# Attention on one core: score blocks in one stream of groups of three, on two PSUM buffers, with the rest of TensorE's work taken from a list

## The chip, the cores and the metric

One core of a Trainium2 chip. The metric is the device time of one execution in microseconds (us), the median over several executions. Before: 136.06 us (135.83 to 136.16). One profiled execution of each kernel gives the trace; its span is about 1.8 us shorter than the time.

## The reference

```python
batch, heads, seq, dim = 8, 8, 512, 64          # float32 q, k, v
scores = np.einsum('bhqd,bhkd->bhqk', q, k) / np.sqrt(dim)
attn = np.exp(scores - scores.max(-1, keepdims=True))
attn = attn / attn.sum(-1, keepdims=True)
return np.einsum('bhqk,bhkd->bhqd', attn, v)
```

There are 64 heads, handled as 32 pairs. Each pair has 8 score blocks of 128 keys x 512 queries (4 chunks of keys, 2 heads). The kernels leave the maximum out and get the sum from a column of ones beside v.

## The kernel before

In the trace TensorE's work stands in the order in which the program is written: four scores from 92.49 us on, 16 value matmuls from 93.48, four transposes from 94.00, and the next scores from 94.32. Per pair, GpSimd casts q, k, v to fp16, TensorE transposes q and k (into tp), and VectorE copies the result to tqk. Then TensorE makes scores (st), ScalarE takes the exponential (pt; one such instruction is called an activation), TensorE multiplies with v (into the accumulator o), and VectorE normalises (rc, ob). The program puts all that TensorE writes into PSUM memory: three buffers for st, one for tp, one for o.

```python
    ps_st = ... tile_pool(name="ps_st", bufs=3, space=PSUM)   # 3 buffers of 1024 columns
    ps_o  = ... tile_pool(name="ps_o",  bufs=1, space=PSUM)   # 1 buffer
    ps_t  = ... tile_pool(name="ps_t",  bufs=1, space=PSUM)   # 1 buffer
    ...
    def scores(g, half):              # 2 blocks of each head of the pair
        ss = [ps_st.tile([P, 2, S], FP32, tag="st", ...) for h in range(2)]
        # ... four matmuls, each on the 64 rows of its head
        for h in range(2):
            nc.scalar.activation(out=pts[g][h][:, 2*half : 2*half+2, :],
                                 in_=ss[h][:, :, :], func=EXP, scale=scale)
    def values(g, h):                 # 16 matmuls into o, then the normalisation
        o = ps_o.tile([P, NI, D + 1], FP32, tag="o", ...)
        # ... matmuls
        nc.vector.reciprocal(out=rc[:, :, :], in_=o[:, :, D : D + 1])
        nc.vector.tensor_tensor(out=ob[:, h], in0=o[:, :, 0:D],
                                in1=rc[:, :, :].broadcast_to([P, NI, D]), op=AluOp.mult)
    ...
        for g in range(NP):
            load(g + AHEAD); cast(g + 3)
            scores(g + 1, 0)
            values(g, 0)
            transpose(g + 3, 1)
            scores(g + 1, 1)
            values(g, 1)
            transpose(g + 3, 0)
```

The scores of the two heads start almost together: in the trace two at 21.459 and 21.465 us, the next at 21.674.

The softmax here doesn't subtract the row's maximum and nothing guards it: scores larger than these inputs give would overflow.

## Time and profile before

| | before |
|---|---|
| time | 136.06 us |
| span of the profiled run | 134.3 us |
| ScalarE busy | 118.9 us (89%) |
| activations | 128 of 1024 columns |
| activation 4, after eight blocks | starts at 14.43 us |
| last activation | starts at 127.34 us |

To the lines that the prediction shows I add ScalarE's group and all that it waited for. The columns of the first are busy time, mean duration of one in ns, and the idle time in front; those of the second are total wait, number, longest.

```profile
L115 ACT ACTIVATE pt<-st 128x1024 f16<-128x1024 f32 x128 | 117.6, 1261 | 9.0 <-PE st L107 9.0
...
ACT pt L115 <- PE st L107: 9.0, 3, 5.5
```

ScalarE waits three times in the whole run, all before 17 us. After that it is the bound, and only two things can help: fewer microseconds per column on ScalarE, or a shorter head and tail.

### The profile page before, as it was taken

Reading aid. Unit: us, or ns where it says so; the run is one execution under the profiler, and the core shown is the slowest. Engines: PE = TensorE matmul, PEld = TensorE weight load, DVE = VectorE, ACT = ScalarE, POOL = GpSimd, SP = SyncE. Lnnn points to the kernel's source line nnn. Section 1 sums busy time; section 2 is a strip of 40 time slices with the busy share of each in tenths; the row PEclk is TensorE's granted clock in tenths of the full one; section 3 lists DMA queues with packets and bytes.
Section 4 is the critical chain, followed back from the end, with each engine's and each line's share of the span. In section 5 each row is a group of like instructions: output and inputs, shape, how many; then the busy total and the mean of one; then the engine's idle time right before and its main releaser. Section 6 shows DMA issues by size and latency. Waiting matters only on the chain.

```text
span 134.3 us, 3901 instructions
## 1 busy us (share of the span) xinstructions
PE 115.7 (86%) x1536; PEld 61.6 (46%) x1536; DVE 60.4 (45%) x192; ACT 118.9 (89%) x129; POOL 59.9 (45%) x108
## 2 busy tenths in 40 slices
PE   0475999999999999999999999999999999998750
PEld 0223455554445554445554445554445554444340
DVE  0203455445555445554445554445554445553230
ACT  3073599999999999999999999999999999999930
POOL 2578831555355554545516545535537624500000
PEclk9999999999999999999999999999999999999975
DMA  4999937999998999988999969979998879422222
GB/s 127 292 326 358 301 100 230 324 318 267 285 306 293 290 263 295 307 266 302 315 277 284 300 192 307 320 248 314 314 296 305 290 224 289 151 78 78 83 78 78
DMA packets 34835, 33.81 MB, mean 252 GB/s; under 512 B 2049, under 2 KB 34817, under 8 KB 34817
## 3 DMA queue, kind: packets, MB, share of 16 engines
q1 hardware_dynamic: 34816, 33.56, 78.7%
q8 instruction: 12, 0.20, 0.6%
q14 instruction: 7, 0.05, 0.1%
HBM read 25.17 MB, written 8.39 MB: 250 GB/s over the span
## 4 chain that ended last, share of the span: by engine, by line
ACT 64%; issue 15%; PE 12%; DVE 3%; DMA 2%; POOL 0%; ACTq 0%
ACT pt L115 64%; PE st L107 5%; PE o L131 3%; PE tp L92 3%; DMA k<-in_k_dram 2%; DVE tqk L93 2%; DVE ob L140 1%; POOL qkp L78 0%; DVE rc L139 0%; ACTq L115 0%
## 5 line engine op out<-in xcount | busy, mean ns | idle before, releaser
L115 ACT ACTIVATE pt<-st 128x1024 f16<-128x1024 f32 x128 | 117.6, 1261 | 9.0 <-PE st L107 9.0
L107 PE MATMUL st<-tqk 64*128 64x512 f16 x256 | 62.8, 394 | 7.0 <-ACT pt L115 1.6
L131 PEld LDWEIGHTS <-pt 128*128 128x128 f16 x1024 | 36.6, 99 | 28.5 <-DVE tqk L93 24.6
L131 PE MATMUL o<-vp,pt 128*128 128x65 f16 x1024 | 44.5, 196 | 1.6 <-DVE ob L140 1.6
L78 POOL CAST qkp<-k 128x512 f16<-128x512 f32 x32 | 19.6, 613 | 48.8 <-DMA k<-in_k_dram 33.5
L139 DVE RECIPROCAL rc<-o 128x4 f32<-128x4 f32 x64 | 11.6, 182 | 57.1 <-PE o L131 57.1
L93 DVE COPY tqk<-tp 128x512 f16<-128x512 f16 x64 | 26.4, 413 | 11.3 <-PE tp L92 11.3
L92 PE MATMUL tp<-ident,qkp 128*128 128x128 f16 x256 | 26.1, 228 | 6.3 <-POOL qkp L78 4.2
L140 DVE TENSOR_TENSOR ob<-o,rc 128x256 f32<-128x256 f32 x64 | 27.1, 424 | 2.2
L107 PEld LDWEIGHTS <-tqk 64*128 64x128 f16 x256 | 12.3, 94 | 32.5 <-issue 26.4
L83 POOL CAST vp<-v 128x512 f16<-128x512 f32 x32 | 19.7, 616 | 5.8 <-DMA v<-in_v_dram 3.9
L78 POOL CAST qkp<-q 128x512 f16<-128x512 f32 x32 | 19.6, 613 | 2.5 <-DMA q<-in_q_dram 1.9
L92 PEld LDWEIGHTS <-qkp 128*128 128x128 f16 x256 | 16.5, 101 | 7.8 <-POOL qkp L78 4.7
L115 ACT ACT_TABLE_LOAD x1 | 1.3, 1283 | 0.7 <-PEq L194 0.7
masks.py:197 POOL MEMSET ident<- 128x128 f16 x1 | 0.2, 204 | 0.3 <-POOLq L194 0.3
masks.py:199 POOL TENSOR_SCALAR_AFFINE_SELECT ident<-ident 128x128 f16<-128x128 f16 x1 | 0.3, 292 | 0.1
L160 POOL MEMSET vp<- 128x8 f16 x6 | 0.3, 135 | 0.0
L194 POOL MEMSET const-float32-0.0<- 128x1 f32 x1 | 0.1, 98 | 0.2 <-issue 0.2
L194 POOL MEMSET const-bfloat16-1.0<- 128x1 bf16 x1 | 0.1, 101 | 0.0
L194 POOL MEMSET const-uint8-127<- 128x1 uint8 x1 | 0.1, 101 | 0.0
L194 POOL MEMSET const-float32-1.0<- 128x1 f32 x1 | 0.1, 98 | 0.0
## 6 DMA issues: line engine op xcount, KB each, us to landing
k<-in_k_dram SPq DMA_DIRECT2D x32, 256.0 KB, 4.1
q<-in_q_dram SPq DMA_DIRECT2D x32, 256.0 KB, 4.3
v<-in_v_dram SPq DMA_DIRECT2D x32, 256.0 KB, 4.4
out_dram<-ob SPq DMA_DIRECT2D x32, 256.0 KB, 3.2
```

The source lines that it names most:

```text
L78: nc.gpsimd.tensor_copy(out=t[:, n].rearrange("p i (h d) -> p h i d", h=2), in_=tiles[name][:, :, :, :],)
L83: nc.gpsimd.tensor_copy(out=vps[g % NV][:, :, :, 0:D], in_=tiles["v"][:, :, :, :])
L92: nc.tensor.transpose(tp[:, i, :], qkp[g][:, n, i, :], ident)
L93: nc.vector.tensor_copy(out=tqk[g][:, n, :], in_=tp.rearrange("p i c -> p (i c)"))
L107: nc.tensor.matmul(ss[h][:, cc, :], tqk[g][po : po + 64, 1, c * P : (c + 1) * P], tqk[g][po : po + 64, 0, :], start=True, stop=True,)
L115: nc.scalar.activation(out=pts[g][h][:, 2 * half : 2 * half + 2, :], in_=ss[h][:, :, :], func=EXP, scale=scale,)
L131: nc.tensor.matmul(o[:, qc, :], pts[g][h][:, c, qc * P : (qc + 1) * P], vps[g % NV][:, h, c, :], start=(c == 0), stop=(c == NI - 1),)
L139: nc.vector.reciprocal(out=rc[:, :, :], in_=o[:, :, D : D + 1])
L140: nc.vector.tensor_tensor(out=ob[:, h], in0=o[:, :, 0:D], in1=rc[:, :, :].broadcast_to([P, NI, D]), op=AluOp.mult,)
L160: nc.gpsimd.memset(vps[n][:, :, :, D : D + 1], 1.0)
L194: nc = _bacc.Bacc("TRN2", target_bir_lowering=False, num_devices=1)
```

## The change

The intent is to spare ScalarE's fixed cost per instruction: undisturbed activations start 0.903 us apart with 1024 columns (before) and 1.331 us with 1536 (the changed kernel), which can be put as 0.836 ns a column and 47 ns an instruction. The 256 score blocks of all pairs form one stream, cut into groups of three: 86 activations in place of 128. A buffer of scores now has 1536 columns, and there are two of them instead of three of 1024: the same 3072 columns in all. All other TensorE work stands in one list of items (an item is four value matmuls or two transposes), and each step takes some items behind its scores. The first pair's loads and casts are spread over queues and engines, six matmuls on zeros run before the first real ones, meant to end sooner the half rate that TensorE shows at the start (in before the scores are 0.40 us apart until 16.1 us and 0.215 us afterwards), and the last pair takes its value matmuls block by block and is stored by halves.

```diff
+GROUP = 3
+ST_BUFS = 2
+LAG = 2
...
-        for g in range(NP):
-            load(g + AHEAD)
-            cast(g + 3)
-            scores(g + 1, 0)
-            values(g, 0)
-            transpose(g + 3, 1)
-            scores(g + 1, 1)
-            values(g, 1)
-            transpose(g + 3, 0)
+    for g in range(NP):
+        for h in range(2):
+            if g + 2 < NP:
+                for part in range(2):
+                    fill.append((-1, transposes, (g + 2, 1 - h, part)))
+            for part in range(NI):
+                need = NB * g + 2 * (part if g == NP - 1 else NI - 1) + h
+                fill.append((need, values, (g, h, part)))
...
+        for m in range(steps):
+            n0 = m * GROUP
+            if n0 % NB < GROUP:
+                g = n0 // NB
+                load(g + AHEAD)
+                cast(g + 3)
+            scores(m)
+            quota = max(0.0, (n0 + GROUP) * len(fill) / TOTAL)
+            budget = GROUP * 3
+            while done < len(fill) and done < quota and budget > 0:
+                need, what, args = fill[done]
+                if need >= (m - LAG + 1) * GROUP:
+                    break
+                what(*args)
+                done += 1
+                budget -= 1
```

(The spread first pair, the warming matmuls and the handling of the last pair are left out of this cut.)

More of the change, by code (lines that the diff above doesn't have):

```diff
@@ L32 @@
     ppb = H // 2
+    NB = 2 * NI
+    TOTAL = NP * NB
     cpool = ctx.enter_context(tc.tile_pool(name="const", bufs=1))
@@ L37 @@
     tpool = ctx.enter_context(tc.tile_pool(name="tqk", bufs=4))
-    ppool = ctx.enter_context(tc.tile_pool(name="pt", bufs=6))
+    ppool = ctx.enter_context(tc.tile_pool(name="pt", bufs=24 // GROUP))
     opool = ctx.enter_context(tc.tile_pool(name="out", bufs=4))
-    ps_st = ctx.enter_context(tc.tile_pool(name="ps_st", bufs=3, space=bass.MemoryType.PSUM))
+    ps_st = ctx.enter_context(
+        tc.tile_pool(name="ps_st", bufs=ST_BUFS, space=bass.MemoryType.PSUM)
+    )
     ps_o = ctx.enter_context(tc.tile_pool(name="ps_o", bufs=1, space=bass.MemoryType.PSUM))
@@ L46 @@
     ident = cpool.tile([P, P], FP16, name="ident")
+    zeros = cpool.tile([P, S], FP16, name="zeros")
     raw = {}
@@ L50, with source @@
     tqk = {}
-    st = {}
-    pts = {}
-    outs = {}
+    tps = {}
+    blocks = {}
+    os = {}
+    obs = {}
     def where(g):
         return g // ppb, 2 * (g % ppb)
+    def source(src, g):
+        b, h = where(g)
+        return src[b, h : h + 2].rearrange("h (p i) d -> p h i d", i=NI)
     def load(g):
@@ L60, in load @@
             return
-        b, h = where(g)
         tiles = {}
@@ L64, in load, with cast_v @@
             t = lpool.tile([P, 2, NI, D], FP32, tag=f"{name}32", name=f"{name}32_{g}")
-            nc.sync.dma_start(
-                out=t.rearrange("p h i d -> p h (i d)"),
-                in_=src[b, h : h + 2].rearrange("h (p i) d -> p h (i d)", i=NI),
-            )
+            nc.sync.dma_start(out=t[:, :, :, :], in_=source(src, g))
             tiles[name] = t
         raw[g] = tiles
+    def cast_v(g):
+        nc.gpsimd.tensor_copy(out=vps[g % NV][:, :, :, 0:D], in_=raw[g]["v"][:, :, :, :])
     def cast(g):
@@ L74, in cast @@
             return
-        tiles = raw.pop(g)
         t = qpool.tile([P, 2, NI, P], FP16, tag="qkp", name=f"qkp_{g}")
@@ L79, in cast @@
                 out=t[:, n].rearrange("p i (h d) -> p h i d", h=2),
-                in_=tiles[name][:, :, :, :],
+                in_=raw[g][name][:, :, :, :],
             )
         qkp[g] = t
-        nc.gpsimd.tensor_copy(out=vps[g % NV][:, :, :, 0:D], in_=tiles["v"][:, :, :, :])
-    def transpose(g, n):
-        if g >= NP:
-            return
-        if n == 1:
-            tqk[g] = tpool.tile([P, 2, S], FP16, tag="tqk", name=f"tqk_{g}")
-        tp = ps_t.tile([P, NI, P], FP16, tag="tp", name=f"tp_{g}_{n}")
-        for i in range(NI):
-            nc.tensor.transpose(tp[:, i, :], qkp[g][:, n, i, :], ident)
-        nc.vector.tensor_copy(out=tqk[g][:, n, :], in_=tp.rearrange("p i c -> p (i c)"))
@@ L95, in scores @@
-    def scores(g, half):
-        if g >= NP:
-            return
-        if half == 0:
-            pts[g] = [
-                ppool.tile([P, NI, S], FP16, tag="pt", name=f"pt_{g}_{h}") for h in range(2)
-            ]
-        ss = [ps_st.tile([P, 2, S], FP32, tag="st", name=f"st_{g}_{h}_{half}") for h in range(2)]
-        for cc in range(2):
-            c = 2 * half + cc
-            for h in range(2):
-                po = 64 * h
-                nc.tensor.matmul(
-                    ss[h][:, cc, :],
-                    tqk[g][po : po + 64, 1, c * P : (c + 1) * P],
-                    tqk[g][po : po + 64, 0, :],
-                    start=True,
-                    stop=True,
-                )
-        for h in range(2):
-            nc.scalar.activation(
-                out=pts[g][h][:, 2 * half : 2 * half + 2, :],
-                in_=ss[h][:, :, :],
-                func=EXP,
-                scale=scale,
-            )
@@ L122, in values @@
-    def values(g, h):
-        if g < 0:
-            return
-        if h == 0:
-            outs[g] = opool.tile([P, 2, NI, D], FP32, tag="ob", name=f"ob_{g}")
-        ob = outs[g]
-        o = ps_o.tile([P, NI, D + 1], FP32, tag="o", name=f"o_{g}_{h}")
-        for qc in range(NI):
-            for c in range(NI):
-                nc.tensor.matmul(
-                    o[:, qc, :],
-                    pts[g][h][:, c, qc * P : (qc + 1) * P],
-                    vps[g % NV][:, h, c, :],
-                    start=(c == 0),
-                    stop=(c == NI - 1),
-                )
+        cast_v(g)
@@ new lines, in transposes, with scores @@
+    def transposes(g, n, part):
+        if part == 0:
+            if n == 1:
+                tqk[g] = tpool.tile([P, 2, S], FP16, tag="tqk", name=f"tqk_{g}")
+            tps[g] = ps_t.tile([P, NI, P], FP16, tag="tp", name=f"tp_{g}_{n}")
+        tp = tps[g]
+        for i in (2 * part, 2 * part + 1):
+            nc.tensor.transpose(tp[:, i, :], qkp[g][:, n, i, :], ident)
+        if part == 1:
+            nc.vector.tensor_copy(out=tqk[g][:, n, :], in_=tp.rearrange("p i c -> p (i c)"))
+    def scores(m):
+        n0 = m * GROUP
+        size = min(GROUP, TOTAL - n0)
+        st = ps_st.tile([P, GROUP, S], FP32, tag="st", name=f"st_{m}")
+        pt = ppool.tile([P, GROUP, S], FP16, tag="pt", name=f"pt_{m}")
+        for x in range(size):
+            g, j = divmod(n0 + x, NB)
+            c, h = divmod(j, 2)
+            po = 64 * h
+            nc.tensor.matmul(
+                st[:, x, :],
+                tqk[g][po : po + 64, 1, c * P : (c + 1) * P],
+                tqk[g][po : po + 64, 0, :],
+                start=True,
+                stop=True,
+            )
+            blocks[n0 + x] = pt[:, x, :]
+        nc.scalar.activation(
+            out=pt[:, 0:size, :], in_=st[:, 0:size, :], func=EXP, scale=scale
+        )
@@ L138, in values, with normalise @@
+    def normalise(g, h):
+        o = os.pop((g, h))
+        if h == 0:
+            obs[g] = opool.tile([P, 2, NI, D], FP32, tag="ob", name=f"ob_{g}")
+        ob = obs[g]
         rc = opool.tile([P, NI, 1], FP32, tag="rc", name=f"rc_{g}_{h}")
@@ L145, in values @@
         )
-        if h == 1:
-            b, hh = where(g)
-            nc.sync.dma_start(
-                out=out[b, hh : hh + 2].rearrange("h (p i) d -> p h (i d)", i=NI),
-                in_=ob.rearrange("p h i d -> p h (i d)"),
-            )
-            del outs[g], pts[g]
+        last = g == NP - 1
+        if last:
+            nc.sync.dma_start(out=source(out, g)[:, h], in_=ob[:, h])
+        elif h == 1:
+            nc.sync.dma_start(out=source(out, g), in_=ob[:, :, :, :])
+    def values(g, h, part):
+        if part == 0:
+            os[(g, h)] = ps_o.tile([P, NI, D + 1], FP32, tag="o", name=f"o_{g}_{h}")
+        o = os[(g, h)]
+        last = g == NP - 1
+        for x in range(NI):
+            c, qc = (part, x) if last else (x, part)
+            nc.tensor.matmul(
+                o[:, qc, :],
+                blocks[NB * g + 2 * c + h][:, qc * P : (qc + 1) * P],
+                vps[g % NV][:, h, c, :],
+                start=(c == 0 and (qc == 0 or not last)),
+                stop=(c == NI - 1),
+                skip_group_check=last,
+            )
+        if part == NI - 1:
+            normalise(g, h)
@@ new lines, in first_pair @@
+    def first_pair():
+        tiles = {}
+        for name in ("k", "q", "v"):
+            tiles[name] = lpool.tile([P, 2, NI, D], FP32, tag=f"{name}32", name=f"{name}32_0")
+        raw[0] = tiles
+        nc.scalar.dma_start(out=tiles["k"][:, :, 0:2], in_=source(k, 0)[:, :, 0:2])
+        nc.sync.dma_start(out=tiles["q"][:, :, :, :], in_=source(q, 0))
+        nc.sync.dma_start(out=tiles["k"][:, :, 2:4], in_=source(k, 0)[:, :, 2:4])
+        nc.sync.dma_start(out=tiles["v"][:, :, :, :], in_=source(v, 0))
@@ new lines, in first_transposes @@
+    def first_transposes():
+        tiles = raw[0]
+        t = qpool.tile([P, 2, NI, P], FP16, tag="qkp", name="qkp_0")
+        qkp[0] = t
+        k16 = t[:, 1].rearrange("p i (h d) -> p h i d", h=2)
+        q16 = t[:, 0].rearrange("p i (h d) -> p h i d", h=2)
+        nc.vector.tensor_copy(out=k16[:, :, 0:2], in_=tiles["k"][:, :, 0:2])
+        nc.vector.tensor_copy(out=q16[:, 0], in_=tiles["q"][:, 0])
+        nc.scalar.copy(q16[:, 1], tiles["q"][:, 1])
+        nc.gpsimd.tensor_copy(out=k16[:, :, 2:4], in_=tiles["k"][:, :, 2:4])
+        cast_v(0)
+        tqk[0] = tpool.tile([P, 2, S], FP16, tag="tqk", name="tqk_0")
+        tk = ps_t.tile([P, NI, P], FP16, tag="tp", name="tp_0_1")
+        tq = ps_o.tile([P, NI, P], FP16, tag="o", name="tp_0_0")
+        for i in range(2):
+            nc.tensor.transpose(tk[:, i, :], t[:, 1, i, :], ident)
+        nc.vector.tensor_copy(
+            out=tqk[0][:, 1, 0:256], in_=tk[:, 0:2].rearrange("p i c -> p (i c)")
+        )
+        for i in range(NI):
+            nc.tensor.transpose(tq[:, i, :], t[:, 0, i, :], ident)
+        nc.vector.tensor_copy(out=tqk[0][:, 0, :], in_=tq.rearrange("p i c -> p (i c)"))
+        tk2 = ps_t.tile([P, 2, P], FP16, tag="tp", name="tp_0_2")
+        for i in range(2):
+            nc.tensor.transpose(tk2[:, i, :], t[:, 1, 2 + i, :], ident)
+        nc.vector.tensor_copy(
+            out=tqk[0][:, 1, 256:512], in_=tk2.rearrange("p i c -> p (i c)")
+        )
@@ L154 @@
+    fill = []
+    for n in (1, 0):
+        for part in range(2):
+            fill.append((-1, transposes, (1, n, part)))
+    for g in range(NP):
+        for h in range(2):
+            if g + 2 < NP:
+                for part in range(2):
+                    fill.append((-1, transposes, (g + 2, 1 - h, part)))
+            for part in range(NI):
+                need = NB * g + 2 * (part if g == NP - 1 else NI - 1) + h
+                fill.append((need, values, (g, h, part)))
     AHEAD = 5
@@ L155 @@
     with tc.manual_schedule():
-        for g in range(AHEAD):
+        first_pair()
+        for g in range(1, AHEAD):
             load(g)
+        nc.vector.memset(zeros[:, :], 0.0)
         make_identity(nc, ident)
@@ L160 @@
             nc.gpsimd.memset(vps[n][:, :, :, D : D + 1], 1.0)
-        for g in range(3):
-            cast(g)
-        for g in range(2):
-            transpose(g, 1)
-            transpose(g, 0)
-            if g == 0:
-                scores(0, 0)
-                scores(0, 1)
-        transpose(2, 1)
-        transpose(2, 0)
-        for g in range(NP):
-            load(g + AHEAD)
-            cast(g + 3)
-            scores(g + 1, 0)
-            values(g, 0)
-            transpose(g + 3, 1)
-            scores(g + 1, 1)
-            values(g, 1)
-            transpose(g + 3, 0)
+        warm = ps_st.tile([P, GROUP, S], FP32, tag="st", name="warm")
+        for n in range(6):
+            nc.tensor.matmul(warm[:, 0, :], zeros[:, 0:P], zeros[:, :], start=True, stop=True)
+        first_transposes()
+        cast(1)
+        cast(2)
+        done = 0
+        steps = (TOTAL + GROUP - 1) // GROUP
+        for m in range(steps):
+            n0 = m * GROUP
+            if n0 % NB < GROUP:
[12 more added lines that the diff above has]
+                budget -= 1
+        while done < len(fill):
+            need, what, args = fill[done]
+            what(*args)
+            done += 1
 _INS = ['q', 'k', 'v']
```

## The prediction

> **What bounds the kernel now.** I read the busy shares first, then the slices, the chain of waits, and the timeline of one period and of the tail.
>
> ```profile
> PE 115.7 (86%) x1536; PEld 61.6 (46%) x1536; DVE 60.4 (45%) x192; ACT 118.9 (89%) x129; POOL 59.9 (45%) x108
> PE   0475999999999999999999999999999999998750
> ACT  3073599999999999999999999999999999999930
> ```
>
> ScalarE (the softmax exponentials) is busy in all slices from about 17 us to 128 us. TensorE looks as busy[...]. The chain of waits decides it:
>
> ```profile
> 13.43 0.96 PE st L107 x3
> 16.73 4.69 ACT pt L115 x5
> 40.28 0.15 ACT pt L115
> 40.43 0.77 issue
> 41.20 2.70 ACT pt L115 x3
> 43.95 0.15 ACT pt L115
> 44.10 0.77 issue
> 44.87 2.70 ACT pt L115 x3
> ```
>
> The chain runs on ScalarE alone and repeats every 44.10 - 40.43 = 3.67 us, which is one pair of heads: four activations of 1024 columns, 0.917 us apart. 32 pairs x 3.67 = 117.4 us of the 134.3 us. The rest is a head of about 11 us net of the four early activations, and a tail. An activation takes longer than its spacing, because one overlaps the next:
>
> ```profile
> L115 ACT ACTIVATE pt<-st x128: 1018/1292/1318, 7.5 to 127.3; 128x1024 f16<-128x1024 f32 x128
> L115 ACTq EVENT_SEMAPHORE  x58: 17/17/17, 21.9 to 124.7; - x58
> ```
>
> So a score buffer is free only 1.29 us after its activation starts. In the timeline of one period, look at what lies on TensorE between one group of value matmuls (L131) and the next:
>
> ```profile
> 73.31 0.68 PE L131 MATMUL o<-vp,pt 128*128 128x65 f16 x16
> 73.83 0.38 PE L92 MATMUL tp<-ident,qkp 128*128 128x128 f16 x4
> 74.03 0.18 DVE L139 RECIPROCAL rc<-o 128x4 f32<-128x4 f32 x1 [0.86 <-PE o L131]
> 74.15 1.06 PE L107 MATMUL st<-tqk 64*128 64x512 f16 x4
> 74.25 0.42 DVE L140 TENSOR_TENSOR ob<-o,rc 128x256 f32<-128x256 f32 x1
> ```
>
> The output accumulator o has one PSUM buffer. VectorE gives it back at 74.25 + 0.42 = 74.67; until then TensorE does four transposes and the scores, and the next values come at 75.14. The wait is there but covered. In the tail, where nothing lies between, it shows:
>
> ```profile
> 128.92 0.42 DVE L140 TENSOR_TENSOR ob<-o,rc 128x256 f32<-128x256 f32 x1
> 129.39 0.90 PEld L131 LDWEIGHTS <-pt 128*128 128x128 f16 x16 [0.86 <-DVE ob L140]
> ```
>
> [...] single spacings here are 0.903, 0.904, 0.940 and 0.920 us; [...] and the longer ones have a second wait in front. [...] Here 512-column scores are 0.40 us apart until 16.1 us and 0.215 us afterwards.
>
> **The change part by part.** *Grouping.* 128 activations become 85 of 1536 columns and one of 512. The spacing c is [...] 1.345 us per three blocks, 8/3 x 1.345 = 3.59 us per pair against 3.67. Gain: 32 x 0.08 = 2.6 us, if ScalarE never waits.
>
> *Two buffers.* [...] TensorE follows 0.05 us later (in before an activation ends at 74.57 and the waiting matmul starts at 74.63). Scores m+2 so start 1.78 us after activation m. Three blocks in two row groups take two slots: the last starts 0.215 us in and lasts 0.37; with 0.1 us of semaphores the data stand 0.685 us after the first score matmul starts. 1.78 + 0.685 = 2.47 against 2c = 2.69: slack 0.22 us. Two buffers alone are enough, barely.
>
> *Order of the rest on TensorE.* The new loop puts work between score groups from one list, values only if their blocks are two groups old. Counting it out, that condition binds in the steady state, not the even quota, so the work comes in bursts. Over eight groups (three pairs) the counts are 0, 9, 3, 0, 9, 3, 6, 6 items; the compiled order agrees where I compared it. An item is four value matmuls or two transposes. The burst of nine is: four value items of head 0, two transpose items, three value items of head 1, then the next scores. Between the two heads there are now only four transposes (0.22 us), no scores. Timed from the first score matmul of the burst's group: scores hold TensorE 0.52 us (0.215, then 0.305 to the next weight load, as at 73.01 to 73.31); 16 value matmuls, the last starting 0.49 later; 0.23 to the reciprocal and 0.64 to the end of the multiply (73.80, 74.03, 74.67); 0.06 to resume; 12 value matmuls at 33 ns are 0.39; 0.04 to turn round. Sum 2.37 us, of which about 0.67 is waiting for o. With 0.685 the next data stand at 3.06 us. ScalarE needs them 3c - 1.78 = 2.26 us after the same moment. It loses 0.80 us per burst. It cannot win this back, since it is the bound. Steps with 6, 3 or 0 items end in time: six is 0.52 + 0.52 + 0.22 + 0.05 = 1.31 < c.
>
> There are 21 bursts, 20 before the last full group: 20 x 0.80 = 16.0 us.
>
> *Head.* The first k half and q, cast on VectorE and ScalarE, should bring the first activation from 7.50 to about 6.3 us. But all of pair 1's transposes and half of pair 2's stand before scores 2, and k of pair 2 was cast only at 9.80 us in before, with the same bytes ahead of it. So scores 2 come at about 10.3 and activation 2 at 11.2 us, with six blocks done; before had eight done at 11.3 and then idled to 14.43. With the remaining blocks counted, a gain of about 2 us. The first burst still runs at half rate, as in before until 16.1: I add 1.2 us.
>
> *Tail.* The last output is stored by halves, but before it step 84 holds both heads of pair 30 and the first item of pair 31, with two waits for o. By the same durations the end is 9.6 us after scores 84 start, that is 8.7 after activation 84: 2.83 for pair 30 and 0.7 for one value item and the last score; then the three other items and the normalisation 1.6, the last head's 16 matmuls and normalisation 1.36, and 3.1 for the store (3.2 in before).
>
> *Sum.* 11.2 + 82 x 1.345 (110.3) + 16.0 + 1.2 + 8.7 = 147.4 us of span. Time exceeds the span by 136.06 - 134.3 = 1.8. Predicted: 149 us.
>
> **The rivals.** *A: ScalarE stays back to back* (the intent). The wait for o would have to be covered, or the slack be larger by 0.6 us. Then 147.4 - 16.0 = 131.4, time 133, 2% faster. For it: TensorE has spare time on average (per pair 1.15 scores, 1.05 values, 0.44 transposes, 2.6 of 3.59 us). Against it: the order is fixed and the tail of before shows the wait in the open. *B: two buffers are the wait, at every group*: were the slack of 0.22 us negative by 0.1, each of 86 groups would cost 0.1, 9 us more, time about 157. The measured latency speaks against. *C: the array falls back to half rate* in the gaps of the empty groups; [...] unlikely. *D: input transfers bind.* DMA is 80 to 99% busy in many slices, but loads run five pairs ahead and a longer kernel asks for less: no effect after the head.
>
> **Range and chances.** The loss per burst is 0.80 with about 0.2 either way, 4 us in all; the spacing c may be 0.02 higher, 1.7 us; head and tail 1.5. Range 143.5 to 153.5. Faster by over 2% needs nearly rival A in full: 0.04. Within 2%: a loss of 0.2 to 0.45 per burst: 0.06. Slower: 0.90.
>
> **What would show it.** Right: ScalarE waits on PE st in about 20 places of 0.6 to 1.0 us, two in every eight activations; in each, TensorE's weight loads of the values sit idle 0.5 to 0.7 us behind VectorE's multiply; activations otherwise 1.33 to 1.37 us apart; the first activation near 6.3 us, the third near 11. Wrong: ScalarE without regular gaps (A), equal small gaps at every activation (B), score matmuls 0.4 us apart after 20 us (C). A first activation late because of the casts, or a third one not tied to pair 2's k, would make the head wrong.

## The result, and the profile after

The changed kernel takes 147.93 us (147.57 to 148.62, four runs) against 135.94 us in the same rounds (135.38 to 136.16). The profiled run is the longest of the four. The ratio is 1.0895, 95% interval 1.0842 to 1.0948: 9% slower. Ratios here and below are the mean time of one kernel's fast runs over that of the other's of the same rounds, so not quite the ratio of the medians quoted.

The page of the changed kernel: busy shares, the slices of TensorE and ScalarE, ScalarE's group, and below them ScalarE's waits.

```profile
PE 116.2 (79%) x1542; PEld 62.8 (43%) x1542; DVE 61.3 (42%) x196; ACT 119.0 (81%) x88; POOL 56.5 (39%) x107
...
PE   6776998797888688869779778878886968886670
...
ACT  3269468989889889898988988988989898898510
...
L125 ACT ACTIVATE pt<-st 128x1536 f16<-128x1536 f32 x86 | 117.3, 1447 | 19.7 <-PE st L117 19.7
...
ACT pt L125 <- PE st L117: 19.7, 25, 2.9
```

No engine is full any more. ScalarE, which showed 9 in every slice, now shows 8 and 9 in turn, and waits 25 times for scores.

One burst of nine items, in the timeline of TensorE, VectorE and ScalarE. Columns: start, duration, engine and line, operation, and in brackets the idle time before it with what ended it.

```profile
27.49 0.59 PE L117 MATMUL st<-tqk 64*128 64x512 f16 x3 [0.63 <-ACT pt L125]
...
28.01 0.68 PE L157 MATMUL o<-vp,pt 128*128 128x65 f16 x16
...
28.53 0.38 PE L104 MATMUL tp<-ident,qkp 128*128 128x128 f16 x4
28.73 0.18 DVE L135 RECIPROCAL rc<-o 128x4 f32<-128x4 f32 x1 [1.62 <-PE o L157]
28.95 0.42 DVE L136 TENSOR_TENSOR ob<-o,rc 128x256 f32<-128x256 f32 x1
...
29.43 0.43 PEld L157 LDWEIGHTS <-pt 128*128 128x128 f16 x12 [0.69 <-DVE ob L136]
...
29.92 0.60 PE L117 MATMUL st<-tqk 64*128 64x512 f16 x3
...
30.62 1.45 ACT L125 ACTIVATE pt<-st 128x1536 f16<-128x1536 f32 x1 [0.49 <-PE st L117]
```

Read it downwards: scores, 16 value matmuls of head 0, four transposes, and then TensorE's weight loads stand idle for 0.69 us until VectorE's multiply at 28.95 + 0.42 = 29.37 gives o back. Only then come head 1's values and, behind them, the scores that ScalarE waits for. The same four transposes and the same two VectorE instructions stood in before, but there the scores came before the next values.

Where the 146.8 us of span went, from the starts of the 86 activations in the trace: activation 2 starts at 11.07 us. 82 spacings at 1.336 us (the mean of the 58 undisturbed ones from activation 8 on) are 109.6. 18 of the bursts after that put a longer gap behind them, 0.61 to 0.64 us over that (one 0.87): 11.5. The four gaps behind activations 4 to 7 (3.41, 1.73, 2.39, 2.03 us) exceed it by 4.2. From activation 84 to the end 10.4. Sum 146.8.

### The profile page after: what moved, and what is told of

It is laid out like the page before. It is cut to its first block, busy times and chain, and to the rows that moved or that the text cites. A ratio compares the mean times of both kernels' runs of the same rounds, so it can differ in the third digit from the quotient of the medians.

```text
span 146.8 us, 3899 instructions
## 1 busy us (share of the span) xinstructions
PE 116.2 (79%) x1542; PEld 62.8 (43%) x1542; DVE 61.3 (42%) x196; ACT 119.0 (81%) x88; POOL 56.5 (39%) x107
## 4 chain that ended last, share of the span: by engine, by line
PE 43%; ACT 33%; DVE 11%; issue 9%; DMA 2%; ACTq 0%
ACT pt L125 33%; PE o L157 20%; PE st L117 20%; DVE ob L136 7%; DVE rc L135 3%; DMA k<-in_k_dram 2%; PE tp L104 2%; DVE tqk L106 1%; PE tp L198 0%; DVE tqk L199 0%; PE tp L193 0%; ACTq L125 0%; DVE qkp L184 0%
## 5 line engine op out<-in xcount | busy, mean ns | idle before, releaser
L125 ACT ACTIVATE pt<-st 128x1536 f16<-128x1536 f32 x86 | 117.3, 1447 | 19.7 <-PE st L117 19.7
L117 PE MATMUL st<-tqk 64*128 64x512 f16 x256 | 53.7, 407 | 11.7 <-ACT pt L125 11.5
L157 PE MATMUL o<-vp,pt 128*128 128x65 f16 x1024 | 50.4, 201 | 12.6 <-DVE ob L136 12.6
L157 PEld LDWEIGHTS <-pt 128*128 128x128 f16 x1024 | 39.6, 102 | 45.6 <-DVE ob L136 24.1
L135 DVE RECIPROCAL rc<-o 128x4 f32<-128x4 f32 x64 | 11.7, 183 | 72.6 <-PE o L157 72.6
L90 POOL CAST qkp<-k 128x512 f16<-128x512 f32 x31 | 19.1, 616 | 58.7 <-PE tp L104 54.4
L106 DVE COPY tqk<-tp 128x512 f16<-128x512 f16 x62 | 25.7, 414 | 3.3 <-PE tp L104 3.3
L117 PEld LDWEIGHTS <-tqk 64*128 64x128 f16 x256 | 9.7, 96 | 28.5 <-issue 23.1
L90 POOL CAST qkp<-q 128x512 f16<-128x512 f32 x31 | 19.1, 617 | 1.0 <-DMA q<-in_q_dram 0.7
L104 PEld LDWEIGHTS <-qkp 128*128 128x128 f16 x248 | 15.9, 102 | 2.3 <-POOL qkp L90 2.0
L232 PE MATMUL warm<-zeros 128*128 128x512 f16 x6 | 2.7, 630 | 1.2 <-DVE zeros L226 1.2
L232 PEld LDWEIGHTS <-zeros 128*128 128x128 f16 x6 | 0.7, 138 | 2.3 <-DVE zeros L226 1.2
```

Of the source, the lines that this page charges most:

```text
L90: nc.gpsimd.tensor_copy(out=t[:, n].rearrange("p i (h d) -> p h i d", h=2), in_=raw[g][name][:, :, :, :],)
L104: nc.tensor.transpose(tp[:, i, :], qkp[g][:, n, i, :], ident)
L106: nc.vector.tensor_copy(out=tqk[g][:, n, :], in_=tp.rearrange("p i c -> p (i c)"))
L117: nc.tensor.matmul(st[:, x, :], tqk[g][po : po + 64, 1, c * P : (c + 1) * P], tqk[g][po : po + 64, 0, :], start=True, stop=True,)
L125: nc.scalar.activation(out=pt[:, 0:size, :], in_=st[:, 0:size, :], func=EXP, scale=scale)
L157: nc.tensor.matmul(o[:, qc, :], blocks[NB * g + 2 * c + h][:, qc * P : (qc + 1) * P], vps[g % NV][:, h, c, :], start=(c == 0 and (qc == 0 ...
```

## The experiments

My theory: the list order puts both heads' values into one step and so lays the single accumulator's round, o to VectorE and back, open on ScalarE's path. Rivals: two score buffers are too few; TensorE has too much to do; the spread head or the array at half rate (TensorE's scores 0.40 us apart instead of 0.22) costs the time. There are eleven runs of ten kernels, all with a correct result; no run e7 is on record. The time of before in their rounds is 136.09 us in the median.

| run | what is changed | us | ratio to before (95% interval) |
|---|---|---|---|
| e1 | at most 6 items a step | 139.27 | 1.0247 (1.0191 to 1.0303) |
| e2 | multiply twice | 164.92 | 1.2084 (1.1998 to 1.2170) |
| e3 | first pair not spread | 147.54 | 1.0854 (1.0805 to 1.0904) |
| e4 | e1 with groups of two | 139.27 | 1.0233 (1.0190 to 1.0276) |
| e5 | e1, multiply twice | 158.35 | 1.1670 (1.1594 to 1.1747) |
| e6 | e1, transposes a pair earlier | 134.66 | 0.9899 (0.9851 to 0.9947) |
| e6 again | the same | 134.44 | 0.9874 (0.9830 to 0.9917) |
| e8 | early extra matmuls | 145.21 | 1.0630 (1.0542 to 1.0717) |
| e9 | e6, extra matmuls, spread early steps | 133.46 | 0.9692 (0.9635 to 0.9749) |
| e10 | e9, heads never in one step | 133.25 | 0.9687 (0.9592 to 0.9783) |
| e11 | e6 with groups of two | 137.82 | 1.0135 (1.0104 to 1.0167) |

**e1: at most six items in a step.**

```diff
-            budget = GROUP * 3
+            budget = 6
```

> The changed kernel with at most six items of other TensorE work per step in place of nine; nothing else. If the wait for the one accumulator inside the bursts of nine costs the time (my theory), the scores and transposes come back between the heads, the 20 gaps of about 0.63 us on ScalarE go (20 x 0.63 = 12.6 us), activations stay 1.33 to 1.35 us apart from about 25 us on, and the time falls from 147.9 to 135 to 137 us. If two score buffers are too few, or TensorE has too much work in all, the gaps only move to other steps and the time stays above 145 us.

139.27 us, 8.7 us less than the changed kernel. The gaps of 1.95 and 1.97 us are gone, so the rivals of too few buffers and too much work fall: e1 has the same two buffers and the same matmuls. But the time is over 2 us above the forecast: the spacings now repeat as 1.53, 1.38, 1.42, 1.42, 1.35, 1.47, 1.38, 1.35 us, 11.29 us per eight steps where 8 x 1.336 is 10.69. A second wait had been lying under the first. Timeline of e1:

```profile
72.13 0.37 PE L117 MATMUL st<-tqk 64*128 64x512 f16 x1
72.21 0.42 DVE L136 TENSOR_TENSOR ob<-o,rc 128x256 f32<-128x256 f32 x1
...
72.55 0.42 DVE L106 COPY tqk<-tp 128x512 f16<-128x512 f16 x1
...
73.02 0.39 PE L117 MATMUL st<-tqk 64*128 64x512 f16 x2 [0.52 <-DVE tqk L106]
```

One score matmul of the group runs; the others belong to the next pair, whose transposes TensorE made only in the step before. VectorE copies them to tqk after the normalisation, and the scores wait until 72.55 + 0.42 = 72.97. The list has pair g + 2's transposes beside pair g's values; before had g + 3.

**e2: the multiply of the normalisation twice.**

```diff
         nc.vector.tensor_tensor(out=ob[:, h], in0=o[:, :, 0:D], in1=rc..., op=AluOp.mult)
+        nc.vector.tensor_tensor(out=ob[:, h], in0=o[:, :, 0:D], in1=rc..., op=AluOp.mult)
```

> The changed kernel with the multiply of the normalisation done twice (same result), so that the accumulator is given back 0.42 + 0.03 us later. My theory: each of the 20 bursts loses that 0.45 us more, 9.1 us, and the time is about 157 us, gaps of ScalarE 1.05 to 1.1 us. If the gaps come from late score buffers or from TensorE's total work, the extra VectorE work (61 us busy of 147, 27 more) is hidden and the time stays within 1 us of 148.

164.92 us: 17 us more, not 9. TensorE's waits for o, in the changed kernel and then in e2:

```profile
PE o L157 <- DVE ob L136: 12.6, 23, 0.8
```

```profile
PE o L163 <- DVE ob L142: 29.7, 38, 1.3
```

No wait of the scores for VectorE's copies of the running transposes stands among e2's, so it is the return of o that the longer normalisation delays. But of the two long gaps in eight steps only one grew by the 0.45 foretold, from 1.95 to 2.41 us; the other went from 1.97 to 2.06. What I had left out is that the round is now 0.49 + 0.93 + 0.45 = 1.87 us and so also longer than a step where six items follow six: two spacings that were 1.33 us became 1.52 and 1.88. Eight steps take 13.25 us against 11.94, 1.31 more where I expected 0.9. Over 76 steps that is 12.4 us. Another 2.7 us lie where the array fell back to half rate in mid-run: the windows of e2 read a clock of 0.50 from 98.3 to 101.6 us and from 125.6 to 132.3 us, the scores are 0.40 us apart there, and the longest idle time of TensorE in the 10 us before was 0.97 us. The accumulator's round is the cause; the size of my forecast was wrong for want of these terms.

**e5: e1 with the multiply twice.** The edits of e1 and e2 together.

> e1 with the multiply done twice. From one head's first value matmul to the next head's it then takes 0.49 + 0.93 + 0.45 = 1.87 us, more than the 1.344 of a step. Where four steps with values follow one another that is 3 x 0.53 us less a slack of about 0.5, so about 1.1 us per eight steps, 10 to 12 us more than e1. If the accumulator has nothing to do with it, e1 within 1 us.

158.35 us, 19 more than e1. The 1.88 us stands in the spacings, twice in eight steps, and each eight take 12.86 us against 11.29, that is 1.57 where I expected 1.1. My reading, not tested alone, is that the slack I had counted was already used by the wait for the copies. This run is less clean than e2, for VectorE's second multiply delays the copies too: TensorE's wait for o grew from 2.3 us in e1 to 11.7, but the scores' wait for the copies grew as well, from 9.4 to 16.1.

**e4: e1 with groups of two on three buffers.**

```diff
-GROUP = 3
-ST_BUFS = 2
+GROUP = 2
+ST_BUFS = 3
-            budget = GROUP * 3
+            budget = 6
```

> As e1 with groups of two blocks on three buffers: the grouping of three alone undone, with the stall-free order kept. My theory: ScalarE back to back 0.917 us apart, 128 x 0.917 = 117.4 us against 85.3 x 1.344 = 114.7, so 2.5 to 3 us slower than e1. If the larger activation has no gain per column, equal to e1 within 0.5 us; if three buffers were needed, faster than e1.

The same time as e1, not 2.5 to 3 us more. The spacings repeat as 1.01, 0.92, 0.90, 0.90 us, 3.74 per pair, against e1's 11.29 / 3 = 3.76. Each has its own extra wait, so this run does not weigh the grouping. It had to wait for e6 and e11.

**e6: the transposes one pair earlier.** As e1, and in the list:

```diff
-    for n in (1, 0):
-        for part in range(2):
-            fill.append((-1, transposes, (1, n, part)))
+    for p in (1, 2):
+        for n in (1, 0):
+            for part in range(2):
+                fill.append((-1, transposes, (p, n, part)))
     for g in range(NP):
         for h in range(2):
-            if g + 2 < NP: ...   # two items of pair g + 2, ahead of the values
             for part in range(NI): ...
+            if g + 3 < NP:
+                for part in range(2):
+                    fill.append((-1, transposes, (g + 3, 1 - h, part)))
```

> e1 with each pair's transposes put one pair earlier (three ahead of the values in place of two, each after the value items). In e1 the spacings repeat as 1.53, 1.38, 1.42, 1.42, 1.35, 1.47, 1.38, 1.35 us; where it is 1.53 and 1.47 the score matmul waits for VectorE's copy of transposes made in the same step or just before. Theory: those two fall to 1.42 or less, 0.2 to 0.3 us per eight steps, 2 to 3 us in all, so 136.3 to 137.3; the 1.42 stay, for they are the accumulator's own round (0.49 + 0.93). If the wait is the accumulator's alone, e1 within 0.5 us.

134.66 us, and 134.44 when repeated: 1.0 and 1.3% under before, and better than the forecast. TensorE's waits of e1, and then of e6:

```profile
PE st L117 <- DVE tqk L106: 9.4, 19, 0.7
```

```profile
PE st L117 <- DVE tqk L199: 0.3, 1, 0.3
```

In e1 the scores waited 19 times for copies of the running transposes (L106); in e6 only once for the first pair's own (L199). Seven of eight spacings are 1.33 to 1.35 us, one is 1.42: 10.73 us per eight steps. I was wrong that the others at 1.42 would stay. The round through o is still 1.42 us, as the starts of two successive heads' weight loads in e6 show:

```profile
60.29 0.56 PEld L157 LDWEIGHTS <-pt 128*128 128x128 f16 x16 [0.47 <-DVE ob L136]
...
61.71 0.37 PEld L157 LDWEIGHTS <-pt 128*128 128x128 f16 x10 [0.47 <-DVE ob L136]
```

But it exceeds a step by only 0.08 us; the two empty steps in eight seem to give that back before ScalarE feels more than one spacing of 1.42.

> e6 unchanged, again, for the comparison with e11 in the same rounds and to see whether its 134.66 (1% under before) holds: 134 to 135.3.

**e11: e6 with groups of two on three buffers.** The edit of e4 on e6.

> e6 with groups of two on three buffers: the grouping alone undone where nothing else makes ScalarE wait (which e4 against e1 did not give). Theory: 0.917 us per 1024 columns in place of 1.34 per 1536, 117.4 against 114.6 us of ScalarE, so 2.3 to 3.2 us slower than e6 in the same rounds. If the third buffer covers waits that e6 still has (one of 0.08 us per eight steps, and the early ones), only 0.5 to 2 us slower.

137.82 us against 134.44 for e6, 3.4 us; the ratio of the two ratios, 1.0135 / 0.9874 = 1.026, says 3.5; the forecast was 2.3 to 3.2. Here the grouping has its value. ScalarE needs 114.4 us for the blocks in e6 (56 spacings of its steady part, scaled to 256 blocks) where 128 x 0.917 is 117.4; e11 still has small waits of its own, which would make the rest. The grouping is not quite alone here: e11 also has a third buffer, and as LAG counts groups, values follow their scores after four blocks instead of six. Its TensorE waits 32 times for an activation before value matmuls (11.5 us), which e6's does not, so a part of the 3.4 us may come from that.

**e3: the first pair not spread.**

```diff
-        first_pair()
-        for g in range(1, AHEAD):
+        for g in range(AHEAD):
             load(g)
...
-        first_transposes()
+        cast(0)
+        for n in (1, 0):
+            transposes(0, n, 0)
+            transposes(0, n, 1)
```

> The changed kernel with the first pair loaded, cast and transposed as in before (three whole loads, casts on GpSimd), the warming matmuls kept: the spread first pair alone undone. My theory: activation 0 comes about 0.7 us later (7.5 us), but activation 2 waits for pair 2's k anyway (its cast began at 9.19 us in before and 8.79 in the changed kernel), so it moves by 0.3 to 0.6 us from 11.07 and the time by as much: 148.2 to 148.6. If the spread head were worth its whole gain at activation 0, 0.7 us or more.

147.54 us, below the forecast and no worse than the 147.93 of the changed kernel; the ratios' intervals overlap. Activation 0 comes at 7.50 us in place of 6.88, activation 2 at 11.68 in place of 11.07. I expected such a delay of 0.3 to 0.6 us, but it isn't shown: in the profiled runs of e1, e2 and e5, which start as the changed kernel does, activation 2 comes at 11.31, 12.05 and 11.95 us, so one run differs from the next by more than that. The spread first pair buys nothing that these runs can show.

**e8: four extra matmuls on zeros in the early steps.** Into the buffer of o, which is free then: one before each of two sets of transposes, two after the scores of step 3.

```diff
+                if m < 4 and what is transposes and args in ((1, 0, 0), (2, 1, 0)):
+                    dummy(1, ps_o, "o")
                 what(*args)
...
+            if m == 3:
+                dummy(2, ps_o, "o")
```

> The changed kernel with four extra matmuls on zeros in the first steps, where TensorE stands idle between 7.8 and 13.5 us. In the changed kernel scores are at half rate (0.4 us apart) until about 22 us, in before until 16; gaps 4 to 7 of ScalarE sum to 9.56 us where regular ones with one burst sum to 5.97. Theory: the array comes to full rate near 14 us, these gaps fall to 6 to 7.5 us, and the time falls by 2 to 3.5 us, to 144.5 to 146. If the early gaps are waits for input, no change.

145.21 us, 2.7 less. The gaps behind activations 4 to 7 are 2.65, 1.35, 1.33 and 1.33 us, 6.7 in all. In the changed kernel the array is still at half rate at 20 us, as the chain of waits shows (start, duration):

```profile
20.27 0.96 PE st L117 x3
21.23 1.00 PE o L157 x16
22.66 0.56 PE st L117 x3
```

Three scores take 0.96 us at 20.27 and 0.56 at 22.66. So the half rate behind the early gaps is shown, in size too: they fall from 9.56 to 6.7 us, the time by 2.7.

**e9: e6 with the early matmuls, pair 2's transposes spread, and extra matmuls near the end.**

```diff
-            budget = 6
+            budget = (0, 4, 2, 2)[m] if m < 4 else 6
+            if m >= steps - 6 and m < steps - 2:
+                dummy(2, ps_t, "tp")
```

(with the list of e6 and the edit of e8)

> e6 with the early extra matmuls of e8, with pair 2's transposes spread over steps 2 and 3 so that activation 2 does not wait for pair 2's k (near 10 us in place of 11.1 to 11.3), and with extra matmuls in four of the last six steps so that the array keeps its full rate through the tail. Sum of the theories: e6's 136.8 less 3 (warm), 1 (head), 1.5 (tail): 131 to 133 us, faster than before by 2 to 3.5%. Each part that fails leaves its share.

Four runs: 131.71, 131.90, 135.02, 135.16 us. The two longer ones are over 1.5% above the fastest, so the ratio 0.9692 rests on two runs. The profiled run is a fast one. Activation 2 starts at 9.80 us, against 11.07 to 12.23 in the profiled runs of the changed kernel, e1, e2, e5, e6 and its repeat, so it was the transposes of pair 2, which wait for its k, that held it. The mean granted clock of the profiled run is 0.980, that of the changed kernel's 0.961; that the extra matmuls near the end keep the rate up through the tail is not shown. One long gap of 2.75 us is left near the end, with the familiar line before it:

```profile
117.07 0.30 PEld L157 LDWEIGHTS <-pt 128*128 128x128 f16 x8 [0.86 <-DVE ob L136]
...
118.56 4.14 ACT L125 ACTIVATE pt<-st 128x1536 f16<-128x1536 f32 x3 [1.14 <-PE st L117]
```

There are no transposes left for the last pairs, so even six items hold parts of two heads.

**e10: e9 with the heads never in one step, until the last three steps.**

```diff
+                if what is values and args[2] == 0 and budget < 6 and m < steps - 3:
+                    break
```

> e9 with two heads never in one step, until the last three steps. In e9 one gap of 2.75 us is left on ScalarE, before activation 82, where step 81 holds values of both heads of pair 29, and the weight loads wait 0.86 us for VectorE's multiply. Theory: that gap falls to 1.35 to 1.45, the rest stays: 1.3 us less than e9's quicker runs (131.8), so about 130.5; if the gap has another cause it stays at 2.7.

Six runs, 130.83 to 133.56 us, median 133.25, which is 2.1% under before. Only two are fast (130.83 and 132.65); the profiled run is a slow one. In it the gap of 2.75 us has become 1.58 and 1.59, so the cause of that gap is right, but how much time it saves does not come out of this scatter. e9 and e10 beat before; e10 is not shown to beat e9. Why the runs of these two scatter by over 2% stays open. The two profiled runs give a lead: in e9's, a quick one, scores are 0.22 us apart from 10.2 us on; in e10's, a slow one, they are 0.40 apart at 11.2 and 13.6 us and 0.22 only from 15.9 us on, and activation 8 starts 2.9 us later (20.86 against 17.91). The other runs left no trace that could confirm it.

## Why the prediction was right

The predicted 149.0 us (143.5 to 153.5, slower at 0.90) met 147.93. Point by point:

- **Spacing of the activations:** 1.345 us forecast, an estimate of mine, 1.336 measured. Right. Its reason was not: in it I had put 15 ns on a second wait before nearly every activation, but undisturbed spacings with such a wait are 1.331 us too, as in before activations 12, 16, 20 and 24 have it at 0.903 us. The 1.347 stands behind each gap.
- **The bursts:** the pattern of items, the place of the wait (0.69 us idle in front of head 1's weight loads; forecast 0.67) and its cause are as forecast, and e1 and e2 show that it is the accumulator's round: the gaps go when no step holds nine items, and the wait for o grows with the normalisation. The order on which the reading rests is that of the matmuls in the timeline of the burst (scores at 27.49 us, values at 28.01, transposes at 28.53, values at 29.43, scores at 29.92). The loss behind a burst was mis-sized: 0.80 us forecast, 0.61 to 0.64 measured. The term of the sum that failed is the release of the score buffer: of the 1.78 us from activation m to scores m+2, 1.73 stood for it, an estimate of mine. The activation that frees the buffer of step 12 lasts 1.46 us, and TensorE starts at 27.49, 0.05 later, so each burst began nearly 0.3 us earlier than I had it. (In a full stream the 1.73 us is right: in e6 the records reach 1.68 to 1.76 us.) The turn from values to scores took 0.13 us where I had 0.04 + 0.03, which gave a little back. Of the 20 bursts counted, that of step 4 lies in the half rate at the start, that of step 9 left no gap (1.331 us), and the other 18 cost 11.5 us. The prediction had 16.0 for all 20.
- **The start:** activation 2 at 11.2 forecast, 11.07 measured, and e9 confirms what held it. Activation 0 at 6.3 forecast was 6.88 (6.16 to 6.93 in e1, e2 and e5, which start alike), without an effect that e3 could show.
- **The array at half rate:** 1.2 us was too little. The four early gaps cost 4.2 us, burst 4 included, for which 0.8 + 1.2 = 2.0 stood in the sum. I had taken the end of the half rate from before, "as in before until 16.1", but in this kernel the scores stay 0.40 us apart until 22.6 us. With e8's extra matmuls they are 0.22 apart from 16.5 us on and the loss goes; why the half rate lasts longer here than in before is not shown.
- **The tail:** 8.7 us forecast from activation 84 to the end, 10.4 measured. I had used full-rate durations, and they fit where the rate is full for longer: e8 has the same tail, its clock falls only 3.1 us after activation 84 (here 1.1 us before it), and its tail takes 8.7 us. The windows of the trace of the changed kernel (stretch, its length, busy time and number of instructions by engine, granted clock, DMA share, GB/s) have the clock at half there:

```profile
134.00:136.00 2.00, 1.17 (x6) 0.10 (x2) 0.48 (x2) 2.00 (x2) 0.00 (x0) 0.82 0.27 94
136.00:140.00 4.00, 2.44 (x37) 2.05 (x36) 1.22 (x4) 1.84 (x2) 0.00 (x0) 0.50 0.06 19
140.00:146.80 6.80, 2.53 (x32) 1.68 (x29) 1.21 (x4) 0.60 (x1) 0.00 (x0) 0.50 0.23 80
```

- **The sum:** 147.4 us of span forecast, 146.8 measured. That is closer than the terms, and so close by luck: 3.7 us too much for the later bursts (19 x 0.80 = 15.2 against 11.5), 0.7 for the spacings and 0.1 for the start stand against 2.2 too little for the half rate at the start and 1.7 for the tail.
- **The rivals:** A (ScalarE back to back) did not come, but e6 shows that the order of TensorE's work alone came near it: no more buffers, 134.5 us where A's estimate was 133. B (two buffers too few) is refuted by e6, which has the same two. C (half rate in the gaps) did not come between 23 and 134 us, only before and after. But that it was unlikely was only my estimate, and short gaps alone do not speak against it: e2 has the half rate twice in mid-run (scores 0.40 us apart) with no gap longer than 0.97 us in the 10 us before. There the measurement decides. For D, longer or shorter inputs were not tried; in the changed kernel ScalarE's steady gaps are all put down to scores.

So the expected gain of 2.6 us from the grouping is borne out (3.4 us in e11 against e6, its other differences included), and was covered by a wait that the new order laid open.

## What to carry to other kernels

When an engine's order is written by hand, ask of every single-buffered tile what lies between its last use and its next writing, and keep enough other work of that engine in between: here scores and transposes covered a round of 0.93 us after the last matmul, and transposes alone, 0.22 us, did not. A list with a budget per step looks even but can put both uses side by side, so count out the steps. And when one wait is taken away, look at the next one before judging: the grouping showed nothing in e4 against e1 and 3.4 us in e11 against e6.

## What the traces show of ScalarE's spacings and of the clock records

- Undisturbed spacings are 0.903 us for 1024 columns in before (twenty in a row, up to activation 27) and 1.331 us for 1536 in the changed kernel (1.330 in e6). Taken as a part per column and a fixed part, the difference, 0.428 us for 512 columns, is 0.836 ns a column, and 47 ns an instruction are left. The means (0.917 us in before, 10.73 / 8 = 1.341 us in e6) are larger because they hold the spacings of 0.940 and 0.920 us in before and the one of 1.42 us in e6.
- The first spacing behind a gap is about 17 ns longer: 0.920 us in place of 0.903 in before, 1.347 in place of 1.331 in the changed kernel.
- Records of activations grow along a back-to-back stream. In the changed kernel they read 1445, 1457, 1469, 1482 ns with starts 1.331 us apart, and begin again near 1445 after a gap; in before they go from 1018 to 1318 ns. The duration of a record in a full stream (1.29 us for 1024 columns) is therefore not what it is after a gap (1.02 us), and taking it over misled my sum by nearly 0.3 us.
- In the changed kernel the windows read a clock of 1.00 from 16 to 23.3 us, and three scores from 20.20 us on still take 0.96 us; but the trace has no clock record before 22.65 us, and the view counts such a stretch as 1.00. Where records stand, they fit the pace: in e8 they read 0.50 from 8.3 to 15.0 us, where scores are 0.40 us apart, and 1.00 from 15.1 us on, where they are 0.22 apart.
